# A ninth pair in place of two wide chunks, and x divided by its rms only in finished chunks

## The chip, the cores and the metric

The kernel runs on one core of one Trainium2 chip. The metric is the device time of one execution in microseconds (us), the median of several runs. Five engines matter here: PE (TensorE, matmuls), DVE (VectorE), ACT (ScalarE), POOL (GpSimd) and SP, which only issues DMAs. Each engine works through its own queue in order; semaphores make one engine wait for another.

## What is computed

One layer of a hybrid decoder block: 256 tokens, model width 4096. x is divided by its rms per token and multiplied by a gain per column; one input projection gives 27 column groups (queries, keys, values and gates of two attention mixers); each mixer's output is normalised, multiplied by SiLU of its gate columns, and the two go through an output projection onto the residual.

```
def _rmsnorm(x, g):
    y = x * rsqrt(mean(x * x, axis=-1) + 1e-6)          # one factor per token
    return y * g                                        # one factor per column
h = _rmsnorm(x, norm_g)
proj = h @ w_in                                         # 4096 -> 26 x 512 + 304 columns
q_a, k_a, v_a, z_a, q_b, kc, vc, ksl, vsl, kwn, vwn, z_b, g_b = split(proj)
o_a = dilated_mixture(q_a, k_a, v_a)                    # 16 heads of 128
o_b = nsa(q_b, kc, vc, ksl, vsl, kwn, vwn, sigmoid(g_b))
y = concat(_rmsnorm(o_a, out_g_a) * silu(z_a), _rmsnorm(o_b, out_g_b) * silu(z_b))
out = _rmsnorm(x + y @ w_out, final_g)
```

Since the rms is one factor per token, (x g / rms) @ w equals ((x g) @ w) / rms: the division can be made on x or on a finished column group.

## The kernel before

**Split products.** Every float32 factor is split into a high and a low part; a product is three matmuls (mm3, lines 98 to 100). ACT makes the high part and DVE the low part (split_to, lines 105 to 109). x comes transposed, as 32 k tiles of 128 columns x 256 tokens, in xh and xl.

**Stages.** Stage 1 (run_stream) multiplies x by single column groups, called chunks: a wide chunk has 512 columns and takes 32 k tiles x 2 token halves x 3 = 192 matmuls. Before the change it has five: 20 (kvc), 21 (sel) and 12 (za0), each 512 wide, then kw (256) and vg (304). Weights come in units of 1 MB through three buffers ("stage") and are split two k tiles at a time, for a 512 wide chunk, into three buffers ("split"); the code lets the splits run two such pieces ahead of the matmuls. While chunk 20 runs, x itself is split too (split_x); the squares of x are summed in the four units that follow (square_x), and token_rms makes rstd, the factor 1/rms per token.

**Pairs.** Stage 2 (run_pairs) multiplies two chunks at once by a block scheme with seven instead of eight products, for nine of the sixteen pairs of k tiles (FAST = 1); the other seven are done plainly. A pair so takes 9 x 21 + 7 x 24 = 357 matmuls of 512 columns. The seven products need sums of 128 x 128 blocks of x, made once in stage 1 (sum_blocks, split_sums, run as a task between the matmuls). There are eight pairs; banks go to DRAM through ACT (L473) and accumulating DMAs of POOL (put_sums). The first pair's buffers lie over those of stage 1. In this stage the order of the queues is written out by hand (manual_schedule); elsewhere a planner of the framework orders each queue by priorities and costs of its own.

**Where the division stands.** Chunks 20, 21, 12 and kw are multiplied by rstd as they leave PSUM (evict_away, L586). For all that follows x is loaded a second time (xr), multiplied by the gain and by a row of 1/rms (token_rms_rows: a matmul, L183, spreads rstd over the partitions), its block sums are made from that, and renew_x splits it into xh and xl again during the kw chunk.

**Stage 3** multiplies seven z chunks and the first output chunk, with the attention of both mixers as tasks between the matmuls. A head group of mixer A (attend_a) splits its values, then fetches its keys from DRAM (fetch, tag "qk" with two buffers: the keys take the values' buffer, so SP issues the DMA when the split is done), then transposes queries and keys on PE (L610). The next head group's values and queries are fetched early. attend_b fetches qb0 in start_b and transposes it next.

Of the kernel before, what the change touches and what calls it, by code (L numbers as in the profile page):

```python
# [83 lines left out]
def hybrid_trunk(ctx: ExitStack, tc: tile.TileContext, a: dict):  # L84
# [47 lines left out]
    def load_xT(piece):  # L132
# [4 lines left out]
        t = x_raw[piece] = room["o"].tile([P, G4, SEQ], F32, name="xp", tag="o", bufs=4)  # L137
# [19 lines left out]
    def load_x_nat(i):  # L157
        m, q = divmod(i, 4)
        t = x_nat[i] = room["o"].tile([P, DM // 4], F32, name="xn", tag="o", bufs=4)
        nc.sync.dma_start(t, a["x"][m * P : (m + 1) * P, q * DM // 4 : (q + 1) * DM // 4])  # L160
# [9 lines left out]
    def token_rms():  # L170
        s = room["work"].tile([P, NT], F32, name="ss")
        nc.vector.reduce_sum(s, ssx, axis=AX.X)
        rsqrt_mean(rstd, s, DM)
        dg = K["dg"] = room["work"].tile([P, NT, P], F32, name="dg", tag="xg")
        for m in range(NT):
            nc.vector.tensor_scalar_mul(dg[:, m], ident, rstd[:, m : m + 1])
        K["full"] = room["work"].tile([P, P], F32, name="full", tag="st")
        nc.vector.memset(K["full"], 1.0)

    def token_rms_rows():  # L180

        pr = room["psm"].tile([P, SEQ], F32, name="pr", tag="ps")
        nc.tensor.matmul(pr, K["full"], K["dg"].rearrange("p m t -> p (m t)"), start=True, stop=True)  # L183
        rows = K["rows"] = room["work"].tile([P, 1, SEQ], F32, name="rows", bufs=1)
        nc.scalar.activation(rows[:, 0], pr, AF.Copy)


    xn, sops, x_again = {}, {}, {}
# [6 lines left out]

    def sum_blocks(i):

        q, j = divmod(i, 4)
        if j == 0:
            xn[q] = room["o"].tile([P, 4, 2, SEQ], F32, name="xn", tag="o", bufs=4)  # L200
        if i % 2 == 0:
            t = x_again[i // 2] = room["work"].tile([P, G4, SEQ], F32, name="xr", tag="xr")
            nc.sync.dma_start(t, a["xT"][i // 2])
        t = x_again[i // 2]
        g = room["work"].tile([P, 2, SEQ], F32, name="xg", tag="xg")
        for d in range(2):
            nc.scalar.activation(g[:, d], t[:, 2 * (i % 2) + d], AF.Copy, scale=g_in[:, 2 * i + d : 2 * i + d + 1])
        n = xn[q][:, j]
        nc.vector.tensor_tensor(n, g, K["rows"].to_broadcast([P, 2, SEQ]), op=OP.mult)
        if FAST[i]:  # L210
            a11, a21, a12 = n[:, 0, :P], n[:, 0, P:], n[:, 1, :P]
            a22 = n[:, 1, P:]
            s = room["work"].tile([P, 4, P], F32, name="st", tag="st")
            add_blocks(s, a11, a12, a21, a22)
            sops[i] = s
# [8 lines left out]
    def sums():  # L224
        for i in range(NKP + 1):
            if i < NKP:
                sum_blocks(i)
            if i > 0:
                split_sums(i - 1)
            yield  # L230

    def renew_x(i):

        q, j = divmod(2 * i, QK)
        n = xn[i // 4][:, i % 4]
        split_to(xh[q][:, j : j + 2], xl[q][:, j : j + 2], n)
# [175 lines left out]
    IN_PLACES, IN_BANKS = ("f0", "t", "w", "p", "f1"), ("p6", "p7", "p5", "p4", "p1", "p2", "p3", "e")  # L412
# [163 lines left out]
    def fetch(key, width=CW):  # L576
        t = room["zq"].tile([P, NT, width], F32, name="fetched", tag="qk", bufs=2)
        nc.sync.dma_start(t, scratch(key))
        return t

    def evict_away(key, width=CW, func=AF.Copy, normal=False):

        def done(ps):
            t = room["ev"].tile([P, NT, width], F32, name="away", tag="ev", bufs=3)
            for m in range(NT):
                nc.scalar.activation(t[:, m], ps[m][:, :width], func, scale=1.0 if normal else rstd[:, m : m + 1])  # L586
# [812 lines left out]
```

## Time and profile before

| | |
|---|---|
| median of 3 runs | 1659.88 us (1655.72 to 1660.87) |
| the profiled execution | 1656.62 us, span 1654.8 us |
| PE / DVE / ACT / POOL busy | 98% / 82% / 61% / 8% |
| DMA | 388.04 MB, mean 234 GB/s |

The span reaches from the first to the last instruction of the profiled execution; its own time holds 1.8 us more. Busy PE is modelled (an instruction's end overlaps the next one's start), so paces are read from the starts of instructions.

### The profile page before, as it was taken

How to read it: one execution, taken by the hardware profiler on the slowest of the kernel's cores; microseconds unless marked ns; L12 is line 12 of the kernel's file. 1: busy time of each engine (PE TensorE's matmuls, PEld its weight loads, DVE VectorE, ACT ScalarE, POOL GpSimd, SP SyncE). 2: the span in 40 equal slices, each digit the busy share in tenths (PEclk: the TensorE clock that was granted, in tenths of full speed). 3: DMA queues.
4: the chain of work that ended last, by engine and by line, in shares of the span. 5: the costliest groups of instructions: out<-in, count | busy, mean ns of one | idle time of the engine just before them, and what ended most of it. 6: DMA issues, size and time to landing. Idle time of an engine off the chain costs nothing.

```text
span 1654.8 us, 20979 instructions
## 1 busy us (share of the span) xinstructions
PE 1623.2 (98%) x7772; PEld 1338.6 (81%) x7772; DVE 1354.5 (82%) x1665; ACT 1012.7 (61%) x1291; POOL 138.1 (8%) x183
## 2 busy tenths in 40 slices
PE   9999999999999999999999999999999999999997
PEld 6888978788888888888877787888888878878887
DVE  6586689989898989898966788987866769898984
ACT  6676556665665565656555767676666746656554
POOL 0000000111111111111120000000000000112110
PEclk9999999999999999999999999999999999999999
DMA  9785756979797978887889454544365456798974
GB/s 358 286 317 178 235 200 217 274 245 269 246 270 240 264 254 258 256 258 246 268 294 336 165 205 147 212 140 140 128 211 179 177 200 206 230 271 249 293 284 174
DMA packets 102519, 388.04 MB, mean 234 GB/s; under 512 B 12240, under 2 KB 12880, under 8 KB 88976
## 3 DMA queue, kind: packets, MB, share of 16 engines
q1 hardware_dynamic: 80064, 336.61, 57.6%
q0 software_dynamic: 21920, 49.03, 13.5%
q8 instruction: 61, 1.00, 0.2%
q10 hardware_dynamic: 432, 1.05, 0.2%
q14 instruction: 42, 0.34, 0.1%
HBM read 338.36 MB, written 50.38 MB: 235 GB/s over the span
## 4 chain that ended last, share of the span: by engine, by line
PE 84%; DVE 6%; DMA 3%; issue 3%; ACT 3%; SPq 0%; ACTq 0%; POOLq 0%; POOL 0%; DVEq 0%
PE p L99 14%; PE p L100 13%; PE p L98 13%; PE acc L99 11%; PE acc L100 11%; PE acc L98 10%; PE e L100 2%; PE e L99 2%; PE e L98 2%; DVE bf L459 2%; DMA bw<-in_w_in 1%; DMA w<-in_cmp_v_w 1%; DVE bf L458 1%; DVE bt L452 1%; PE pt L1030 1%
## 5 line engine op out<-in xcount | busy, mean ns | idle before, releaser
L106 DVE TENSOR_TENSOR wl<-w,wh 128x1024 fp32r<-128x1024 f32 (+2 forms) x210 | 246.8, 1178 | 132.0 <-ACT wh L105 131.6
L105 ACT ACTIVATE wh<-w 128x1024 fp32r<-128x1024 f32 (+2 forms) x210 | 214.5, 1024 | 154.6 <-PE acc L100 132.1
L98 PE MATMUL acc<-wh,xh 128*128 128x512 f32 (+2 forms) x768 | 293.8, 383 | 2.6 <-ACT wh L105 2.6
L99 PE MATMUL acc<-wl,xh 128*128 128x512 f32 (+2 forms) x768 | 292.4, 381 | 1.5 <-DVE wl L106 1.5
L100 PE MATMUL acc<-wh,xl 128*128 128x512 f32 (+2 forms) x768 | 291.7, 380 | 0.0
L459 DVE TENSOR_TENSOR bf<-bt,bf 128x2048 fp32r<-128x2048 f32 x99 | 226.1, 2284 | 0.0
L454 ACT ACTIVATE bf<-bt 128x1024 fp32r<-128x1024 f32 x99 | 104.9, 1059 | 170.7 <-DVE bt L452 170.7
L106 DVE TENSOR_TENSOR bp<-bw,bp 128x2048 fp32r<-128x2048 f32 x66 | 151.0, 2288 | 64.8 <-ACT bp L105 64.8
L451 ACT ACTIVATE bf<-bw 128x1536 fp32r<-128x1536 f32 x99 | 147.0, 1485 | 62.4 <-DMA bw<-in_w_in 39.5
L105 ACT ACTIVATE bp<-bw 128x2048 fp32r<-128x2048 f32 x66 | 126.0, 1909 | 78.1 <-PE e L100 63.2
L458 DVE TENSOR_TENSOR bf<-bw,bf 128x1536 fp32r<-128x1536 f32 x99 | 173.3, 1751 | 0.0
L98 PEld LDWEIGHTS acc<-wh,xh 128*128 128x128 f32 x768 | 145.3, 189 | 27.1 <-ACT wh L105 3.8
L99 PEld LDWEIGHTS acc<-wl,xh 128*128 128x128 f32 x768 | 145.4, 189 | 26.7 <-DVE wl L106 3.5
L100 PEld LDWEIGHTS acc<-wh,xl 128*128 128x128 f32 x768 | 145.3, 189 | 24.4
L457 ACT ACTIVATE bf<-bt 128x1024 fp32r<-128x1024 f32 x99 | 105.2, 1063 | 38.7 <-DVE bt L456 37.9
L452 DVE TENSOR_TENSOR bt<-bw 128x1024 f32<-128x1024 f32 x99 | 120.9, 1221 | 9.7 <-DMA bw<-in_w_in 6.5
L99 PE MATMUL p<-bf,sum 128*128 128x512 f32 x288 | 113.2, 393 | 2.9 <-DVE bf L459 2.9
L100 PE MATMUL p<-bf,sum 128*128 128x512 f32 x288 | 112.3, 390 | 0.0
L98 PE MATMUL p<-bf,sum 128*128 128x512 f32 x288 | 112.3, 390 | 0.0
L99 PE MATMUL p<-bp,xh 128*128 128x512 f32 x288 | 112.2, 389 | 0.0
L98 PE MATMUL p<-bp,xh 128*128 128x512 f32 x288 | 112.0, 389 | 0.0
L100 PE MATMUL p<-bp,xl 128*128 128x512 f32 x288 | 112.0, 389 | 0.0
(329 smaller groups left out, 3295.3 us busy)
## 6 DMA issues: line engine op xcount, KB each, us to landing
bw<-in_w_in SPq DMA_DIRECT2D x256, 512.0 KB, 6.1
w<-in_w_in SPq DMA_DIRECT2D x76, 1024.0 KB, 5.0
bw<-in_w_out SPq DMA_DIRECT2D x96, 512.0 KB, 5.1
w<-in_w_out SPq DMA_DIRECT2D x16, 1024.0 KB, 5.0
scr_q<-parts POOLq DMA_DIRECT2D x30, 256.0 KB, 7.3
scr_k<-parts POOLq DMA_DIRECT2D x30, 256.0 KB, 7.7
scr_v<-parts POOLq DMA_DIRECT2D x30, 256.0 KB, 7.7
scr_qb<-parts POOLq DMA_DIRECT2D x30, 256.0 KB, 8.9
```

Of the source, the lines that this page charges most:

```text
L98: nc.tensor.matmul(out, lh, rh, start=start, stop=False)
L99: nc.tensor.matmul(out, lh, rl, start=False, stop=False)
L100: nc.tensor.matmul(out, ll, rh, start=False, stop=stop)
L105: nc.scalar.activation(h, src, AF.Copy)
L106: nc.vector.tensor_sub(l, src, h.bitcast(F32))
L451: nc.scalar.activation(h[:, :3], w[:, B22:], AF.Copy)
L452: nc.vector.tensor_tensor(t[:, T3 : T1 + 1], w[:, B22 : B11 + 1], w[:, B12 : B12 + 1].to_broadcast([P, 2, CW]), op=OP.subtract)
L454: nc.scalar.activation(h[:, 3:5], t[:, T3 : T1 + 1], AF.Copy)
L457: nc.scalar.activation(h[:, 5:], t[:, T2:], AF.Copy)
L458: nc.vector.tensor_sub(l[:, :3], w[:, B22:], h[:, :3].bitcast(F32))
L459: nc.vector.tensor_sub(l[:, 3:], t, h[:, 3:].bitcast(F32))
L1030: nc.tensor.transpose(pt[:rows, j], src, ident)
```

## The change

Stage 1 keeps only the chunks 20, kw and vg; 21 and 12 become a ninth pair, the last of stage 2. x is no longer renewed: xh and xl stay x times gain, without the division, in all stages. The block sums are made from the first load of x (x_raw, now with eight buffers) while chunk 20 runs, by one ACT and four DVE instructions for each of the nine fast k pairs; the second load, the spreading matmul and renew_x go away. The division moves to the finished chunks: queries, keys and sel are multiplied by rstd on POOL after they are fetched (divide=True: two instructions of 128 x 512 each, for 13 fetches), values in split_values, z chunks inside the Silu, vg at its eviction. za0, which used to pass Silu in stage 1, passes it in gate after its fetch. The pace of the tasks, the order of PSUM banks and the place of token_rms change with it.

```
--- before.py
+++ after.py
@@ -134,7 +134,7 @@
         if half == 0:
             xh.append(big.tile([P, QK, SEQ], F32R, name=f"xh{q}", tag="x", bufs=8))
             xl.append(big.tile([P, QK, SEQ], F32R, name=f"xl{q}", tag="x", bufs=8))
-        t = x_raw[piece] = room["o"].tile([P, G4, SEQ], F32, name="xp", tag="o", bufs=4)
+        t = x_raw[piece] = room["o"].tile([P, G4, SEQ], F32, name="xp", tag="o", bufs=8)
         if piece == 0:
             nc.sync.dma_start(g_in, a["norm_g"])
             for j, e in ((0, 1), (1, 2), (2, 4)):
@@ -156,7 +156,7 @@
 
     def load_x_nat(i):
         m, q = divmod(i, 4)
-        t = x_nat[i] = room["o"].tile([P, DM // 4], F32, name="xn", tag="o", bufs=4)
+        t = x_nat[i] = room["work"].tile([P, DM // 4], F32, name="xn", tag="xn", bufs=4)
         nc.sync.dma_start(t, a["x"][m * P : (m + 1) * P, q * DM // 4 : (q + 1) * DM // 4])
 
     def square_x(i):
@@ -171,21 +171,9 @@
         s = room["work"].tile([P, NT], F32, name="ss")
         nc.vector.reduce_sum(s, ssx, axis=AX.X)
         rsqrt_mean(rstd, s, DM)
-        dg = K["dg"] = room["work"].tile([P, NT, P], F32, name="dg", tag="xg")
-        for m in range(NT):
-            nc.vector.tensor_scalar_mul(dg[:, m], ident, rstd[:, m : m + 1])
-        K["full"] = room["work"].tile([P, P], F32, name="full", tag="st")
-        nc.vector.memset(K["full"], 1.0)
-
-    def token_rms_rows():
-
-        pr = room["psm"].tile([P, SEQ], F32, name="pr", tag="ps")
-        nc.tensor.matmul(pr, K["full"], K["dg"].rearrange("p m t -> p (m t)"), start=True, stop=True)
-        rows = K["rows"] = room["work"].tile([P, 1, SEQ], F32, name="rows", bufs=1)
-        nc.scalar.activation(rows[:, 0], pr, AF.Copy)
-
-
-    xn, sops, x_again = {}, {}, {}
+
+
+    sops = {}
 
     def add_blocks(s, a11, a12, a21, a22):
         nc.vector.scalar_tensor_tensor(s[:, 0], a21, -1.0, a22, op0=OP.mult, op1=OP.subtract)
@@ -193,26 +181,22 @@
         nc.vector.tensor_tensor(s[:, 2], a11, a21, op=OP.subtract)
         nc.vector.tensor_tensor(s[:, 3], a12, s[:, 1], op=OP.subtract)
 
+    minus_g = cst.tile([P, KT], F32, name="minus_g")
+
     def sum_blocks(i):
 
-        q, j = divmod(i, 4)
-        if j == 0:
-            xn[q] = room["o"].tile([P, 4, 2, SEQ], F32, name="xn", tag="o", bufs=4)
-        if i % 2 == 0:
-            t = x_again[i // 2] = room["work"].tile([P, G4, SEQ], F32, name="xr", tag="xr")
-            nc.sync.dma_start(t, a["xT"][i // 2])
-        t = x_again[i // 2]
-        g = room["work"].tile([P, 2, SEQ], F32, name="xg", tag="xg")
-        for d in range(2):
-            nc.scalar.activation(g[:, d], t[:, 2 * (i % 2) + d], AF.Copy, scale=g_in[:, 2 * i + d : 2 * i + d + 1])
-        n = xn[q][:, j]
-        nc.vector.tensor_tensor(n, g, K["rows"].to_broadcast([P, 2, SEQ]), op=OP.mult)
-        if FAST[i]:
-            a11, a21, a12 = n[:, 0, :P], n[:, 0, P:], n[:, 1, :P]
-            a22 = n[:, 1, P:]
-            s = room["work"].tile([P, 4, P], F32, name="st", tag="st")
-            add_blocks(s, a11, a12, a21, a22)
-            sops[i] = s
+        if not FAST[i]:
+            return
+        k = 2 * i
+        r1, r2 = x_raw[i // 2][:, k % G4], x_raw[i // 2][:, k % G4 + 1]
+        a22 = room["work"].tile([P, P], F32, name="a22", tag="a22")
+        nc.scalar.activation(a22, r2[:, P:], AF.Copy, scale=g_in[:, k + 1 : k + 2])
+        s = sops[i] = room["work"].tile([P, 4, P], F32, name="st", tag="st")
+        m1 = minus_g[:, k : k + 1]
+        nc.vector.scalar_tensor_tensor(s[:, 0], r1[:, P:], m1, a22, op0=OP.mult, op1=OP.subtract)
+        nc.vector.scalar_tensor_tensor(s[:, 1], r1[:, :P], m1, s[:, 0], op0=OP.mult, op1=OP.subtract)
+        nc.vector.tensor_tensor(s[:, 2], a22, s[:, 1], op=OP.subtract)
+        nc.vector.scalar_tensor_tensor(s[:, 3], r2[:, :P], g_in[:, k + 1 : k + 2], s[:, 1], op0=OP.mult, op1=OP.subtract)
 
     def split_sums(i):
         if FAST[i]:
@@ -222,18 +206,14 @@
             sops[i] = t
 
     def sums():
-        for i in range(NKP + 1):
-            if i < NKP:
-                sum_blocks(i)
-            if i > 0:
-                split_sums(i - 1)
-            yield
-
-    def renew_x(i):
-
-        q, j = divmod(2 * i, QK)
-        n = xn[i // 4][:, i % 4]
-        split_to(xh[q][:, j : j + 2], xl[q][:, j : j + 2], n)
+        nc.vector.tensor_scalar_mul(minus_g, g_in, -1.0)
+        fast = [i for i in range(NKP) if FAST[i]]
+        for n in range(len(fast) + 1):
+            if n < len(fast):
+                sum_blocks(fast[n])
+            if n > 0:
+                split_sums(fast[n - 1])
+            yield
 
 
     tasks = deque()
@@ -409,7 +389,7 @@
 
     B12, B22, B11, B21 = range(4)
     T3, T1, T2, T4 = range(4)
-    IN_PLACES, IN_BANKS = ("f0", "t", "w", "p", "f1"), ("p6", "p7", "p5", "p4", "p1", "p2", "p3", "e")
+    IN_PLACES, IN_BANKS = ("f0", "t", "w", "p", "f1"), ("p5", "p1", "p2", "p4", "p6", "p7", "p3", "e")
     OUT_PLACES, OUT_BANKS = ("f1", "t", "p", "f0", "w"), ("p7", "p1", "p6", "p5", "p4", "p2", "p3", "e")
 
     def run_pairs(w_src, dcs, lhs_of, sops, begin, places, names, out=False):
@@ -573,17 +553,19 @@
             scr[key] = dram.tile([P, NT, width], F32, name=f"scr_{key}")
         return scr[key]
 
-    def fetch(key, width=CW):
+    def fetch(key, width=CW, divide=False):
         t = room["zq"].tile([P, NT, width], F32, name="fetched", tag="qk", bufs=2)
         nc.sync.dma_start(t, scratch(key))
+        for m in range(NT if divide else 0):
+            nc.gpsimd.tensor_scalar_mul(t[:, m], t[:, m], rstd[:, m : m + 1])
         return t
 
-    def evict_away(key, width=CW, func=AF.Copy, normal=False):
+    def evict_away(key, width=CW):
 
         def done(ps):
             t = room["ev"].tile([P, NT, width], F32, name="away", tag="ev", bufs=3)
             for m in range(NT):
-                nc.scalar.activation(t[:, m], ps[m][:, :width], func, scale=1.0 if normal else rstd[:, m : m + 1])
+                nc.scalar.activation(t[:, m], ps[m][:, :width], AF.Copy, scale=rstd[:, m : m + 1])
             nc.sync.dma_start(scratch(key, width), t)
         return done
 
@@ -591,7 +573,7 @@
 
         v = room["work"].tile([P, NT, 4, 2, HD], F32R, name="va", tag="n", bufs=2)
         for m in range(NT):
-            split_to(v[:, m, :, 0], v[:, m, :, 1], src[:, m].rearrange("p (j d) -> p j d", j=4))
+            split_to(v[:, m, :, 0], v[:, m, :, 1], src[:, m].rearrange("p (j d) -> p j d", j=4), rstd[:, m : m + 1])
         return v
 
     def transposed(src, key, scale=None):
@@ -645,14 +627,14 @@
     def attend_a(hg):
         vsrc, qsrc = st.pop("va"), st.pop("qa")
         v = split_values(vsrc)
-        ksrc = fetch(f"k{hg}")
+        ksrc = fetch(f"k{hg}", divide=True)
         yield
         yield from transposed(qsrc, "qa", SCALE)
         yield from transposed(ksrc, "ka")
         if hg < 3:
-            st["va"], st["qa"] = fetch(f"v{hg + 1}"), fetch(f"q{hg + 1}")
+            st["va"], st["qa"] = fetch(f"v{hg + 1}"), fetch(f"q{hg + 1}", divide=True)
         else:
-            st["sel"], st["kw"] = fetch("sel"), fetch("kw", 2 * HD)
+            st["sel"], st["kw"] = fetch("sel", divide=True), fetch("kw", 2 * HD)
         qh, ql = st["qaT"]
         kh, kl = st["kaT"]
         o_tiles("a")
@@ -730,6 +712,9 @@
                 nc.sync.dma_start(sz[m], scratch(f"z{which}{i}")[:, m])
             yield
             yield
+            if (which, i) == ("a", 0):
+                for m in range(NT):
+                    nc.scalar.activation(sz[m], sz[m], AF.Silu, scale=rstd[:, m : m + 1])
         for m in range(NT):
             ys = o_at(which, i * CW, CW)[:, m]
             nc.vector.scalar_tensor_tensor(ys, ys, r[:, m : m + 1], sz[m], op0=OP.mult, op1=OP.mult)
@@ -747,7 +732,7 @@
         def done(ps):
             sz = [room["zq"].tile([P, CW], F32, name="sz", tag="zt", bufs=4) for m in range(NT)]
             for m in range(NT):
-                nc.scalar.activation(sz[m], ps[m], AF.Silu)
+                nc.scalar.activation(sz[m], ps[m], AF.Silu, scale=rstd[:, m : m + 1])
             if which in finished:
                 tasks.appendleft(gate(which, i, sz))
             else:
@@ -812,7 +797,7 @@
                 nc.tensor.transpose(pt[:, g, m], t[:, m, c0 : c0 + HD], ident)
         nc.scalar.activation(tT, pt, AF.Copy)
         if which == 1:
-            st["va"], st["qa"] = fetch("v0"), fetch("q0")
+            st["va"], st["qa"] = fetch("v0"), fetch("q0", divide=True)
         pe = room["work"].tile([P, CBL], F32, name="pe", tag="pe", bufs=2)
         nc.sync.dma_start(pe, a[f"cmp_{n}_pe"])
         w2 = room["zq"].tile([P, 2, HD], F32, name="w2", tag="zt", bufs=4)
@@ -935,7 +920,7 @@
         yield
         put_v(0, sel[:, :, 2 * HD :])
         yield
-        st["qb"] = fetch("qb0")
+        st["qb"] = fetch("qb0", divide=True)
         put_v(1, vg[:, :, : 2 * HD])
         g2 = B["gates"]
         nc.scalar.activation(g2, vg[:, :, 2 * HD :], AF.Exp, scale=-1.0)
@@ -946,7 +931,7 @@
     def attend_b(hg):
         yield from transposed(st.pop("qb"), "qb", SCALE)
         if hg < 3:
-            st["qb"] = fetch(f"qb{hg + 1}")
+            st["qb"] = fetch(f"qb{hg + 1}", divide=True)
         first, second = attend_half(hg, 0), attend_half(hg, 1)
         for _ in range(5):
             next(first)
@@ -1209,19 +1194,15 @@
         room[name] = opened(inner, name, n)
 
     room["apart"].tile([P, 3 * HID], F32, name="apart")
-    psum = banks(4, 3, 1)
+    psum = banks(6, 1, 1)
     room["first"] = True
     first_ps, last_ps = [], []
-    pace = 0.5
-    add_chunk(w_chunk(20), CW, x_lhs, first_ps.extend)
-    add_chunk(w_chunk(21), CW, x_lhs, evict_away("sel"), pace=pace)
-    add_chunk(w_chunk(12), CW, x_lhs, evict_away("za0", func=AF.Silu), pace=pace)
-    add_chunk([a["w_kw"][g] for g in range(4)], 2 * HD, x_lhs, evict_away("kw", 2 * HD))
-    add_chunk([a["w_vg"][g] for g in range(8)], 2 * HD + NGATE, x_lhs, last_ps.extend)
-    hooks[1, 17] = token_rms
-    hooks[1, 20] = lambda: (token_rms_rows(), evict_away("kvc")(first_ps), tasks.append(sums()))
-    for i in range(NKP):
-        hooks[3, 2 * i + 1] = lambda i=i: renew_x(i)
+    add_chunk(w_chunk(20), CW, x_lhs, first_ps.extend, pace=0.4)
+    add_chunk([a["w_kw"][g] for g in range(4)], 2 * HD, x_lhs, evict_away("kw", 2 * HD), pace=0.8)
+    add_chunk([a["w_vg"][g] for g in range(8)], 2 * HD + NGATE, x_lhs, last_ps.extend, pace=0.8)
+    hooks[0, 14] = lambda: tasks.append(sums())
+    hooks[1, 26] = token_rms
+    hooks[1, 28] = lambda: evict_away("kvc")(first_ps)
     run_stream()
     while tasks:
         advance()
@@ -1231,7 +1212,7 @@
     room["pairs"] = opened(inner, "pairs", 1)
 
     def begin_pairs():
-        evict_away("vg", 2 * HD + NGATE, normal=True)(last_ps)
+        evict_away("vg", 2 * HD + NGATE)(last_ps)
         psum.close()
         room["banks"] = opened(psum, "banks", 1, space=PS)
         right.close()
@@ -1242,6 +1223,7 @@
         for n, c in (("q", 0), ("k", 4), ("v", 8)):
             dcs.append(((c + i, c + i + 1), (f"{n}{i}", f"{n}{i + 1}")))
         dcs.append(((16 + i, 17 + i), (f"qb{i}", f"qb{i + 1}")))
+    dcs.append(((21, 12), ("sel", "za0")))
     ordered = ExitStack()
     ordered.enter_context(tc.manual_schedule())
     rest = run_pairs(a["w_in"], dcs, x_lhs, sops, begin_pairs, IN_PLACES, IN_BANKS)
```

## Rows read from the trace of the kernel before

**Rows 1.** The page, busy time of PE.
```profile
PE 1623.2 (98%) x7772; PEld 1338.6 (81%) x7772; DVE 1354.5 (82%) x1665; ACT 1012.7 (61%) x1291; POOL 138.1 (8%) x183
```
**Rows 2.** What PE waited for, whole span: total us, times, longest.
```profile
PE p L99 <- DVE bf L459: 5.4, 5, 1.2
```
**Rows 3.** Busy time by stretch in stage 1: stretch, length, engines, clock, DMA.
```profile
30.00:40.00 10.00, 10.00 (x45) 8.02 (x44) 7.22 (x12) 6.78 (x11) 0.00 (x0) 1.00 0.98 390
40.00:50.00 10.00, 10.00 (x44) 8.07 (x43) 7.08 (x11) 5.80 (x10) 0.00 (x0) 1.00 0.82 305
50.00:60.00 10.00, 10.00 (x44) 8.03 (x44) 4.59 (x4) 6.82 (x10) 0.00 (x0) 1.00 0.97 364
...
90.00:100.00 10.00, 10.00 (x45) 8.02 (x44) 9.88 (x23) 9.01 (x16) 0.00 (x0) 1.00 0.82 272
```
**Rows 4.** PE in order of time: last of chunk 12, kw, pairs.
```profile
144.68 0.40 PE L98 MATMUL acc<-wh,xh 128*128 128x512 f32 x1
...
147.96 0.40 PE L100 MATMUL acc<-wh,xl 128*128 128x512 f32 x1
148.19 0.28 PE L98 MATMUL acc<-wh,xh 128*128 128x256 f32 x1
...
197.86 0.40 PE L98 MATMUL p<-bf,xh 128*128 128x512 f32 x1
```
**Rows 5.** ACT in order of time: a pair's last bank leaves PSUM.
```profile
281.77 0.60 ACT L473 ACTIVATE parts<-e 128x512 f32<-128x512 f32 x1 [0.34 <-PE e L100]
...
365.58 0.60 ACT L473 ACTIVATE parts<-e 128x512 f32<-128x512 f32 x1 [0.76 <-PE e L100]
...
446.53 0.60 ACT L473 ACTIVATE parts<-e 128x512 f32<-128x512 f32 x1 [0.76 <-PE e L100]
```
**Rows 6.** PE's groups in the first 240 us: the spreading matmul.
```profile
L183 PE MATMUL pr<-dg,full 128*128 128x256 f32 x2 | 0.6, 380 | 0.0
```
**Rows 7.** DVE's groups by form, first 200 us: one sum, its split.
```profile
L106 DVE TENSOR_TENSOR sum<-st,sum 128x512 fp32r<-128x512 f32 x9 | 6.2, 687 | 1.0 <-ACT sum L105 0.8
...
L191 DVE SCALAR_TENSOR_TENSOR st<-xn 128x128 f32<-128x128 f32 x9 | 2.5, 283 | 0.0
```
**Rows 8.** One piece of chunk 20 being split: ACT, then DVE.
```profile
35.50 1.06 ACT L105 ACTIVATE wh<-w 128x1024 fp32r<-128x1024 f32 x1 [0.55 <-PE acc L100]
...
36.59 1.22 DVE L106 TENSOR_TENSOR wl<-w,wh 128x1024 fp32r<-128x1024 f32 x1 [0.39 <-ACT wh L105]
```
**Rows 9.** SP's fetch issues, and PE's transposes of what was fetched.
```profile
950.98 0.32 SPq L578 DMA_DIRECT2D fetched<-scr_k  x1
...
954.90 1.04 PE L610 MATMUL pt<-ident,fetched 128*128 128x128 f32 x8
...
999.87 0.33 SPq L578 DMA_DIRECT2D fetched<-scr_k  x1
...
1006.17 1.03 PE L610 MATMUL pt<-ident,fetched 128*128 128x128 f32 x8
...
1043.59 0.42 SPq L578 DMA_DIRECT2D fetched<-scr_qb  x1
...
1050.06 1.06 PE L610 MATMUL pt<-ident,fetched 128*128 128x128 f32 x8
```
**Rows 10.** DMA issues: count, size, median us from issue to landing.
```profile
fetched<-scr_k SPq DMA_DIRECT2D x4, 512.0 KB, 3.4
fetched<-scr_qb SPq DMA_DIRECT2D x4, 512.0 KB, 5.5
```
**Rows 11.** POOL's groups by form, whole span: its arithmetic on two elements.
```profile
L115 POOL TENSOR_TENSOR roa<-rsq,nhalf 128x2 f32<-128x2 f32 x1 | 0.7, 722 | 152.8 <-DVE rsq L114 152.8
```
**Rows 12.** Busy time by stretch in stage 3, columns as in rows 3.
```profile
940.00:960.00 20.00, 19.89 (x114) 16.75 (x115) 17.91 (x42) 17.23 (x34) 0.00 (x0) 1.00 0.57 202
...
1040.00:1060.00 20.00, 19.88 (x106) 16.53 (x104) 19.47 (x51) 11.59 (x28) 0.00 (x0) 1.00 0.85 307
```

## The prediction

> **What bounds the kernel now.** I read the page first: PE is busy 98% of the span [rows 1], and no other engine comes near. Busy PE is a model, so I looked next at what PE waited for: its largest group of waits is 5.4 us in five pieces [rows 2], nothing against 1655 us. So time moves when PE gets fewer matmuls, or when something new makes it wait. The views by stretch and by order of time then give the price of each. In stage 1 PE has no idle time after the first 16 us, while DVE stands between 4.59 and 9.88 of 10 us [rows 3]; in 90 to 100, where the block sums are made, DVE is full and PE still does not wait. The reader should take from this that a full DVE alone costs nothing here as long as the splits stay ahead of PE.
>
> **Two chunks become a pair.** Two wide chunks are 384 matmuls. From 144.68 to 147.96 are 14 steps, 0.2343 us each [rows 4], so they take 384 x 0.2343 = 90.0 us, and stage 1 gets that much shorter. A pair in full swing takes 446.53 - 365.58 = 80.95 us from one last bank to the next [rows 5]. That is 357 matmuls of 0.2268 us: the pair saves 27 matmuls, and each one of its own is 0.0075 us quicker than in stage 1, for whatever reason. The ninth pair comes last and finds the others running, so I price it at 80.95. What it does on ACT (sums, evictions), POOL (16 accumulating DMAs) and DVE lies inside that period already. Gain 90.0 - 80.95 = 9.0 us. If it ran at stage 1's pace it would be 357 x 0.2343 = 83.6 us, and the gain 6.4. The first pair took 281.77 - 197.86 = 83.9 us [rows 4, 5], so entering stage 2 costs some 3 us. The new layout of stage 1's buffers under the first pair's may change that by as much either way; the last of them that PE reads are the split buffers, as before, so I take no change.
>
> **What goes away with the renewal.** The spreading matmul is 0.6 us of busy PE at most [rows 6]; with its overlap I take 0.4. The second load of x, 32 gain activations, 16 multiplications by the row and 16 renewing splits ran beside a PE that did not wait, so they are worth nothing. The sums keep their four DVE instructions and their split; only the place changes. Together 9.4 us.
>
> **The sums in chunk 20.** They start behind k tile 14. Chunk 20 ends at 148.19 - 90.0 - 0.4 = 57.8, 17 tiles of 6 x 0.2343 = 1.41 us earlier is 33.9 us. A sum costs DVE 4 x 0.283 + 0.687 = 1.82 us [rows 7], and at a pace of 0.4 about eight of nine come before 57.8: 14.6 us. DVE's idle time there is 6.1 x 0.28 + 10 x 0.29 + 7.8 x 0.54 = 8.8 us [rows 3]. So it is over by 5.8 us at worst. The splits have a lead: a piece whose buffer PE left at 35.5 is done at 37.8 [rows 8], and PE wants it two pieces of 2.81 us behind that, at 41.1, 3.3 us later. So PE loses at most 2.5 us. At least it loses nothing, since means of such short instructions hold the overlap with the next, and the planner may put splits first, as it did at 90 to 100 [rows 3]. I take 0.5, near the lower end, for that row. What waits behind a late split is PE's piece and nothing else; DVE has recovered in kw, where no x is split. token_rms and the eviction of kvc now stand in kw; the squares they wait for come from the four units of kw, as long as those of chunk 21, so I see nothing late.
>
> **POOL multiplies what was fetched.** This is the part that can cost. The fetched keys of a head group are wanted by PE as they land: issue 950.98, landing after 3.4 us at 954.4, transposes at 954.90, a slack of 0.5 us; the third head group repeats this. For the fourth it is 999.87 + 3.4 = 1003.3 against 1006.17, 2.9 us; for qb0 1043.59 + 5.5 = 1049.1 against 1050.06, 1.0 us [rows 9, 10]. The first head group's keys have more, and the other eight divided fetches are issued a head group ahead. At these four places two POOL instructions of time T now stand between landing and PE. Behind them in POOL's queue are other such multiplications and a small pow; POOL's bank DMAs of the last pair stand ahead, as now. The loss, if PE's order stays as it is, is L(T) = 2 max(0, 2T - 0.5) + max(0, 2T - 2.9) + max(0, 2T - 1.0).
>
> T is not in the trace. POOL's arithmetic on 2 elements takes 0.72 us [rows 11], a lower bound; DVE's on 128 x 512 takes 0.69 [rows 7], so 0.72 + 0.69 = 1.41 when POOL is as fast by element as DVE. If it must also wait for one DVE split of 1.22 [rows 8] it is 2.63. L is 2.3 at 0.72, 4.0 at 1.0, 6.5 at 1.41 and 16.1 at 2.63. I take T = 1.0, between the two bare ends. Below all this is nothing: stage 3 is ordered by the planner, which knows of the new instructions and can put matmuls of the z chunk before the transposes. I take half of 4.0, 2.0 us.
>
> [...]
>
> DVE and POOL could also get in each other's way: DVE is busy 17.91 of 20 us in 940 to 960 and 19.47 in 1040 to 1060 [rows 12]; four POOL instructions fall in each. At 0.7 us for each meeting DVE has 2.8 us more to do against 2.1 and 0.5 idle, so this adds up to 3 us of DVE time, and PE's lead covers some. I leave it in the range. [...] Before the change POOL did almost no arithmetic, so the trace cannot say. [...]
>
> za0's Silu adds two activations and a change of ACT's table and back to a stretch where ACT is busy 11.59 of 20 us [rows 12]; the eight idle us hide it. The factor in split_values, the z chunks and vg adds no instruction.
>
> **Sum.** -9.4 + 0.5 + 2.0 = -6.9 us: span 1654.8 to 1647.9, the profiled execution 1656.6 to 1649.7. The median of the three runs is 3.3 us above that execution, so the median forecast is 1659.9 - 6.9 = 1653.0.
>
> **The rivals.** First, nothing is lost: the planner hides POOL, and chunk 20 holds. Then -9.4, 1650.5. For it speaks that PE did not wait in stage 3 for any fetch; against it the slack of 0.5.
>
> Second, the gain goes to POOL's waits: PE's order stays, and T is 1.0 to 2.3. At T = 1.41 it is -9.4 + 0.5 + 6.5 = -2.4, 1657.5: no change. For it speaks that PE takes the keys right behind their landing.
>
> Third, slower: POOL's multiplication is held up by DVE's instructions each time. The sum passes +5 us when L passes 13.9, at 8T - 4.9 = 13.9, T = 2.35. At 2.63 it is -8.9 + 16.1 = +7.2, 1667.1. Against it: only two places have no slack, and not every moment of DVE is a split.
>
> Fourth, the change saves less because the ninth pair runs at stage 1's pace: -9.4 + 2.6 + 2.5 = -4.3, 1655.6.
>
> **How the numbers follow.** About 0.3%, 5 us, is what a measurement of this kernel can tell from no change. Chances: the forecast (-5 to -8.5) 0.42, nothing lost 0.20, POOL's waits on PE's path 0.25, the slower pair 0.05, slower 0.08. Faster gets the first two, 0.62; same 0.30; slower 0.08. The likeliest case's own range is 1651.4 to 1655. The whole range reaches down to nothing lost with 3 us of the entry into stage 2, 1647.5, and up to POOL's waits with T near 1.8 (L = 9.5, +0.6), 1660.5.
>
> **What would show it.** The step of a pair stays 80.95 for the ninth; stage 2 begins 90 us earlier, near 107.5; in 34 to 58 DVE is at 9 of 10 or more and PE's starts stay 0.234 apart, or show gaps up to 2.5 us in all; in stage 3 PE waits for POOL at the second and third head group and at qb0, in all 1 to 4 us; POOL's multiplications take 0.7 to 1.4 us. The prediction is wrong if POOL's instructions take over 2 us, if chunk 20 stalls by more than 3 us, or if entering stage 2 costs more than 6 us.

## The result, and the profile after

The changed kernel takes 1671.72 us (median of 4 runs, 1671.26 to 1676.31) against 1657.8 us for the kernel before in the same measurement: ratio 1.0086, 95% interval 1.0069 to 1.0102. It is slower by 14 us. The forecast was 1653.0, with 1660.5 as the upper end of the range: wrong in sign and outside the range.

The profiled execution is the longest of the four (1676.31 us, span 1674.4). Its page, line of the engines, answers to [rows 1]: PE's busy share fell by one point, POOL's rose from 8 to 12%.

```profile
PE 1621.6 (97%) x7743; PEld 1334.6 (80%) x7743; DVE 1375.1 (82%) x1651; ACT 1011.5 (60%) x1259; POOL 197.4 (12%) x224
```

What PE waited for (total us, times, longest) has a new first line. Against [rows 2]:

```profile
PE pt L592 <- POOL fetched L560: 12.0, 8, 2.7
PE p L99 <- DVE bf L439: 7.7, 7, 1.2
PE ph L842 <- DVE bhl L106: 5.6, 2, 3.0
PE acc L99 <- DVE wl L106: 4.1, 6, 1.5
PE acc L98 <- ACT wh L105: 4.0, 3, 1.8
```

The places of the landmarks show where to look. In order of time, the last bank of the eighth and of the ninth input pair and of the first output pair leave through ACT (the rows that answer to [rows 5]):

```profile
766.52 0.60 ACT L453 ACTIVATE parts<-e 128x512 f32<-128x512 f32 x1 [0.51 <-PE e L100]
847.48 0.60 ACT L453 ACTIVATE parts<-e 128x512 f32<-128x512 f32 x1 [0.76 <-PE e L100]
1449.82 0.60 ACT L453 ACTIVATE parts<-e 128x512 f32<-128x512 f32 x1 [0.37 <-PE e L100]
```

In the kernel before, the same output bank:

```profile
1431.78 0.60 ACT L473 ACTIVATE parts<-e 128x512 f32<-128x512 f32 x1 [0.76 <-PE e L100]
```

The ninth pair takes 847.48 - 766.52 = 80.96 us. Stage 2 ended at 852.05 before and ends at 847.48 now: 4.6 us are gained up to there, and in the other kernels below that keep this part, 6 to 10. From there to the end of the first output pair, which I call stage 3, it is 1431.78 - 852.05 = 579.7 us before and 602.3 now. Of what was lost, 22.6 us was lost in stage 3; behind its end 1.6 us more go (1674.4 - 1449.82 = 224.6 us against 1654.8 - 1431.78 = 223.0).

In stage 1 the block sums did what was hoped for. The stretches while chunk 20 runs with the block sums in it (columns as in [rows 3]): DVE is full, PE does not wait.

```profile
30.00:40.00 10.00, 10.00 (x44) 8.04 (x43) 10.00 (x21) 8.28 (x17) 0.00 (x0) 1.00 0.94 358
40.00:50.00 10.00, 10.00 (x45) 8.03 (x44) 9.75 (x22) 9.07 (x17) 0.00 (x0) 1.00 0.72 264
50.00:60.00 10.00, 10.00 (x47) 8.16 (x46) 9.96 (x21) 7.52 (x13) 0.00 (x0) 1.00 0.90 338
```

Stage 3 is where POOL now stands between a landed tile and PE. POOL's multiplications (ns, shortest/median/longest; first and last start):

```profile
L560 POOL TENSOR_SCALAR fetched<-fetched,rstd x26: 1557/1568/3647, 889.4 to 1117.2; 128x512 f32<-128x512 f32 x26
```

Around the second head group's keys POOL's queue and then PE's show the chain. The keys land, POOL needs 3.98 us for its two instructions, and PE's transposes (L592) follow each of them, with one matmul of the z chunk (951.74) between:

```profile
949.14 3.98 POOL L560 TENSOR_SCALAR fetched<-fetched,rstd 128x512 f32<-128x512 f32 x2 [16.91 <-DMA fetched<-scr_k]
```

```profile
948.93 0.39 PE L100 MATMUL acc<-wh,xl 128*128 128x512 f32 x1
951.54 0.44 PE L592 MATMUL pt<-ident,fetched 128*128 128x128 f32 x2 [2.22 <-POOL fetched L560]
951.74 0.48 PE L98 MATMUL acc<-wh,xh 128*128 128x512 f32 x1
953.17 1.05 PE L592 MATMUL pt<-ident,fetched 128*128 128x128 f32 x6 [0.96 <-POOL fetched L560]
...
955.52 0.63 PE L99 MATMUL acc<-wl,xh 128*128 128x512 f32 x1
955.94 0.63 PE L100 MATMUL acc<-wh,xl 128*128 128x512 f32 x1
956.37 0.63 PE L98 MATMUL acc<-wh,xh 128*128 128x512 f32 x1
956.80 0.56 PE L99 MATMUL acc<-wl,xh 128*128 128x512 f32 x1
957.19 0.40 PE L100 MATMUL acc<-wh,xl 128*128 128x512 f32 x1
```

The reader is to see a second thing here: behind the wait, matmuls of 512 columns start 0.42 us apart instead of 0.234. From 954.0 to 957.2, where they stand, the granted clock is 0.51; from 957.2 to 960, where such matmuls start 0.23 us apart again, it is 1.00. In the windows around the four places (clock in the third column from the end) the granted clock is below 1 in three of them.

```profile
950.00:960.00 10.00, 7.50 (x32) 6.15 (x33) 5.19 (x9) 2.98 (x6) 4.46 (x3) 0.83 0.60 188
980.00:990.00 10.00, 7.12 (x37) 5.41 (x36) 4.03 (x5) 3.81 (x6) 3.19 (x2) 1.00 0.69 243
1010.00:1020.00 10.00, 7.68 (x34) 5.98 (x33) 4.30 (x8) 3.50 (x9) 6.76 (x4) 0.83 0.62 196
1060.00:1070.00 10.00, 6.70 (x24) 5.66 (x25) 5.30 (x10) 3.19 (x4) 7.14 (x5) 0.66 0.61 206
```

That is 1.7 + 1.7 + 3.4 = 6.8 us of full clock taken away in these windows, a part of them while PE waited anyway.

### The profile page after: what moved, and what is told of

It reads as the page before. It is cut to its first block, busy times and chain, and to the rows that moved or that the text cites. A ratio compares the mean times of both kernels' runs of the same rounds, so it can differ in the third digit from the quotient of the medians.

```text
span 1674.4 us, 20936 instructions
## 1 busy us (share of the span) xinstructions
PE 1621.6 (97%) x7743; PEld 1334.6 (80%) x7743; DVE 1375.1 (82%) x1651; ACT 1011.5 (60%) x1259; POOL 197.4 (12%) x224
## 4 chain that ended last, share of the span: by engine, by line
PE 74%; DVE 10%; DMA 6%; issue 5%; ACT 3%; POOL 1%; SPq 0%; ACTq 0%; POOLq 0%; DVEq 0%
PE p L99 14%; PE p L100 13%; PE p L98 13%; PE acc L99 8%; PE acc L100 7%; PE acc L98 7%; DMA bw<-in_w_in 3%; DVE bf L439 2%; PE e L100 2%; PE e L99 2%; PE e L98 2%; DVE bf L438 2%; DVE bt L432 1%; DVE wl L106 1%; DMA w<-in_cmp_v_w 1%
## 5 line engine op out<-in xcount | busy, mean ns | idle before, releaser
L106 DVE TENSOR_TENSOR wl<-w,wh 128x1024 fp32r<-128x1024 f32 (+2 forms) x178 | 209.0, 1176 | 111.1 <-ACT wh L105 110.5
L105 ACT ACTIVATE wh<-w 128x1024 fp32r<-128x1024 f32 (+2 forms) x178 | 180.6, 1018 | 128.4 <-PE acc L100 100.7
L98 PE MATMUL acc<-wh,xh 128*128 128x512 f32 (+2 forms) x640 | 243.3, 382 | 4.0 <-ACT wh L105 4.0
L99 PE MATMUL acc<-wl,xh 128*128 128x512 f32 (+2 forms) x640 | 242.7, 379 | 4.2 <-DVE wl L106 4.1
L100 PE MATMUL acc<-wh,xl 128*128 128x512 f32 (+2 forms) x640 | 241.4, 377 | 0.0
L99 PEld LDWEIGHTS acc<-wl,xh 128*128 128x128 f32 x640 | 122.1, 191 | 23.9 <-DVE wl L106 7.2
L98 PEld LDWEIGHTS acc<-wh,xh 128*128 128x128 f32 x640 | 121.8, 191 | 22.8 <-ACT wh L105 5.5
L100 PEld LDWEIGHTS acc<-wh,xl 128*128 128x128 f32 x640 | 121.7, 190 | 18.7
L99 PE MATMUL p<-bf,sum 128*128 128x512 f32 x324 | 127.7, 394 | 5.3 <-DVE bf L439 5.2
L98 PE MATMUL p<-bf,sum 128*128 128x512 f32 x324 | 126.3, 390 | 0.0
L100 PE MATMUL p<-bf,sum 128*128 128x512 f32 x324 | 126.2, 390 | 0.0
L99 PE MATMUL p<-bp,xh 128*128 128x512 f32 x324 | 126.1, 389 | 0.0
L98 PE MATMUL p<-bp,xh 128*128 128x512 f32 x324 | 126.0, 389 | 0.0
```

The costliest lines, as they stand in the source:

```text
L98: nc.tensor.matmul(out, lh, rh, start=start, stop=False)
L99: nc.tensor.matmul(out, lh, rl, start=False, stop=False)
L100: nc.tensor.matmul(out, ll, rh, start=False, stop=stop)
L105: nc.scalar.activation(h, src, AF.Copy)
L106: nc.vector.tensor_sub(l, src, h.bitcast(F32))
```

## The experiments

Three theories stood in the expectations. P: PE waits for POOL's product of keys and qb0, and loses what follows each wait. C: POOL's reads of SBUF hold up DVE wherever they stand. N: the ninth pair or the new stage 1 is what got slower. "The changed kernel" is the base of each edit.

For all kernels together: the median, the ratio to the kernel before (95% interval), and of one profiled execution each the end of stage 2, the length of stage 3, PE's waits in stage 3 (sum of that view), and the time the low clock took there (for each 10 us of stage 3, 10 x (1 - granted clock), summed). All times in us. Kernels were measured in several rounds, each beside the kernel before; "by the ratios" below is the difference of two ratios times 1658 us. Outside stage 2 the planner orders the queues anew for every kernel, so a difference of a few us between two of them can also be its order; no run holds that order fixed.

```
kernel            median   ratio                    end 2  stage 3  waits  clock
before            1657.8                            852.1   579.7   11.2    3.4
changed           1671.72  1.0086 [1.0069, 1.0102]  847.5   602.3   26.7    8.7
e1_no_divide      1654.98  0.9985 [0.9972, 0.9998]  843.9   582.9   12.9    3.4
e2_act_divide     1654.03  0.9974 [0.9960, 0.9989]  843.8   582.2   13.8    1.7
e3_dve_divide     1651.8   0.9966 [0.9953, 0.9979]  843.8   581.7   13.2    3.5
e4_keys_early     1662.9   1.0027 [1.0011, 1.0042]  843.6   589.1   17.7    3.4
e5_early_qb_dve   1656.24  0.9985 [0.9976, 0.9995]  842.3   585.3   15.4    1.7
e6_eight_pairs    1661.35  1.0021 [1.0011, 1.0030]  853.3   584.7   13.5    6.8
e7_qb_dve         1667.99  1.0058 [1.0043, 1.0073]  844.5   596.1   22.8    6.8
e8_early_dve      1659.18  1.0003 [0.9992, 1.0014]  843.8   588.4   16.2    6.8
e9_path_dve       1656.79  0.9991 [0.9980, 1.0001]  844.7   589.4   16.2    8.5
e10_keys_twice    1676.13  1.0108 [1.0094, 1.0122]  844.0   606.1   28.9   12.0
e11_fill          1677.12  1.0104 [1.0086, 1.0122]  843.6   608.2   23.0    8.5
e12_pool_beside   1655.34  0.9982 [0.9971, 0.9992]  845.7   585.7   15.1    5.1
```

**e1, e2, e3: no multiplication, or one on another engine.** e1 drops the two lines; e2 and e3 change the engine:

```
-            nc.gpsimd.tensor_scalar_mul(t[:, m], t[:, m], rstd[:, m : m + 1])
+            nc.scalar.activation(t[:, m], t[:, m], AF.Copy, scale=rstd[:, m : m + 1])     # e2
+            nc.vector.tensor_scalar_mul(t[:, m], t[:, m], rstd[:, m : m + 1])             # e3
```

> The changed kernel without the 26 POOL multiplications: queries, keys and sel stay undivided, which this kernel leaves out; all else as changed. Theory P (PE waits for POOL's product of keys and qb0, 12.0 us in the changed kernel, and what follows each wait): stage 3 gets as short as before the change, the time falls to 1649 to 1654 us, below the kernel before. Rival N (stage 1 or the ninth pair is what got slower): it stays at 1664 or more. Rival C (POOL's reads hold up DVE wherever they stand) expects the same fall as P here; e4 tells it from P.

> The multiplications move from POOL to ACT, two activations with a scale per fetch, about 0.7 us each. P: the path from landing to PE keeps 1.4 us in place of 3.2 to 4, plus ACT's queue, which is some two thirds full; 1653 to 1661 us, between e1 and the changed kernel. C: as e1, since POOL is idle: 1649 to 1654. N: 1664 or more.

> The multiplications move to DVE, two instructions of 128x512 per fetch, 0.4 to 0.7 us each. P: the path from landing to PE keeps 0.8 to 1.4 us plus DVE's queue, which is nearly full in that stretch; 1653 to 1662 us. C: 1649 to 1656. N: 1664 or more.

All three come out below the kernel before, e3 at 1651.8 lowest. Of P's ranges, e1 lies 1.0 us above its own, e2 in its own and e3 1.2 us below. From the changed kernel to e3 it is 19.9 us, by 26 instructions that moved. N falls: stage 1 and the nine pairs are the same in all of them. In e3 the multiplications take a third of the time:

```profile
L560 DVE TENSOR_SCALAR fetched<-fetched,rstd x26: 469/480/489, 887.1 to 1114.8; 128x512 f32<-128x512 f32 x26
```

and two of the four windows above read, with PE at 9.77 and 10.00 of 10 and the full clock:

```profile
950.00:960.00 10.00, 9.77 (x53) 7.71 (x52) 8.61 (x26) 6.17 (x12) 0.00 (x0) 1.00 0.52 200
1060.00:1070.00 10.00, 10.00 (x57) 8.39 (x56) 9.96 (x33) 9.07 (x20) 0.00 (x0) 1.00 0.24 97
```

That e1, which does less, is not below e3 (the intervals overlap) shows that the multiplications themselves cost nothing measurable on DVE. They do not yet tell P from C, since in all three POOL multiplies nothing.

**e4, e5: POOL multiplies, but a head group ahead.** Keys and queries are fetched and multiplied one head group early and the values take the late place; e5 has qb0 on DVE besides.

```
     def attend_a(hg):
-        vsrc, qsrc = st.pop("va"), st.pop("qa")
-        v = split_values(vsrc)
-        ksrc = fetch(f"k{hg}", divide=True)
-        yield
+        qsrc, ksrc = st.pop("qa"), st.pop("ka")
         yield from transposed(qsrc, "qa", SCALE)
+        vsrc = fetch(f"v{hg}")
         yield from transposed(ksrc, "ka")
...
+        yield
+        v = split_values(vsrc)
+        if hg < 3:
+            st["ka"] = fetch(f"k{hg + 1}", divide=True)
...
+            (nc.vector if key == "qb0" else nc.gpsimd).tensor_scalar_mul(t[:, m], t[:, m], rstd[:, m : m + 1])   # e5
```

> POOL still makes all 26 multiplications, but of each head group the keys and queries are fetched a head group ahead, with the same two buffers, and the values, which POOL does not touch, come on the path in their place; in start_b sel is used before kw, so that qb0 is fetched earlier. P: PE's waits for POOL fall from 12.0 us to under 3, and the time to 1649 to 1657 us. C: POOL's reads still meet DVE's, the time stays at 1662 or more. N: 1664 or more.

> As e4_keys_early (keys and queries fetched a head group ahead and multiplied by POOL), but qb0, for whose product by POOL PE still waited 3.4 us there, is multiplied by DVE; 24 of the 26 multiplications stay on POOL, all off PE's path. Theory P (only what PE waits for costs): the time falls to e3's, 1650 to 1656 us. Rival C (POOL's reads hold up DVE wherever they stand): it stays at 1658 or more, as e4.

e4 falls to 1662.9, 8.8 us below the changed kernel. By its time that is C's range (1662 or more) and not P's; its waits for POOL fell as P had it, nearly (3.4 us, under 3 expected), and are those of qb0 alone:

```profile
PE pt L592 <- POOL fetched L560: 3.4, 2, 2.5
```

In e5 they are gone, and with 24 of 26 multiplications still on POOL the median is 1656.24, below the kernel before. That is 0.2 us above P's range and 1.8 below C's: the place in the chain is most of what costs, as P has it, while by C 24 of 26 parts of the 17 to 20 us would have stayed. e8 below shows where the rest of e4 comes from.

**e7, e9: DVE for a part of the path, in the changed order.** e7 moves qb0 alone to DVE, e9 all that PE takes as it lands (k0 to k3 and qb0); the other 16 stay on POOL.

```
+            (nc.vector if key == "qb0" else nc.gpsimd).tensor_scalar_mul(...)                        # e7
+            (nc.vector if key[0] == "k" or key == "qb0" else nc.gpsimd).tensor_scalar_mul(...)       # e9
```

> The changed kernel with one fetch altered: qb0 is multiplied by DVE, the other twelve by POOL, keys on PE's path as changed. P: what qb0 costs goes, a wait of some 4 us and the slow clock behind it, 3 us more: 1662 to 1667 us; the three waits for keys stay. C: two POOL instructions of 26 fewer, 1669 to 1672 us.

> The changed kernel with DVE for the five fetches whose product PE waits for (the keys of four head groups and qb0), and POOL for the other eight (queries, sel, later qb), 16 instructions. Order of fetches as changed. Theory P (only the products on PE's path cost): as e3, 1650 to 1655 us. Rival C (POOL's reads hold up DVE wherever they stand): 16 of 26 of the loss of 17 to 20 us stays, 1660 or more.

qb0 alone gives 3.7 us (4.6 by the ratios, whose intervals overlap a little), 1.0 us above P's range and 1.0 below C's; in the changed kernel PE's starts at qb0 lose 4.0 us against their usual steps. The waits for POOL go from 12.0 to 7.2 us, but the clock still fell behind 1064 (3.4 us). e9 gives 14.9 us. No wait for POOL is left in it; the largest new one is

```profile
PE s L98 <- ACT kaT L105: 2.8, 1, 2.8
```

and the clock takes 8.5 us, more than in e3. Its median stays 5.0 us above e3's, between P's range and C's. What makes these 5 us was not separated: 3.0 us of waits and 5.0 of low clock fill them in the profile.

**e8: the early order with everything on DVE.** The order of e4, the engine of e3.

> Both remedies: keys and queries fetched a head group ahead, and all divisions on DVE. P: little is left to win over e3, 1649 to 1654 us. C says nothing here, since POOL is idle. A third reading, that the values now on the path are late, would show as 1655 or more.

P's range is missed and the third reading's met. At 1659.18 it is 7.4 us slower than e3 (6.1 by the ratios), and no quicker than e5, which has 24 of the 26 on POOL. The early order therefore has a price of its own, without any POOL: PE waits 2.6 us once for ACT's oT and 3.6 us for DVE's n. So the remainder of e4 and e5 above e3 need not be POOL's: at this order e4, with all 26 on POOL, is 3.7 us above e8 (intervals overlap), with 3.4 us of waits for POOL.

**e10: the keys multiplied twice.**

```
+            if key[0] == "k":
+                nc.gpsimd.tensor_scalar_mul(t[:, m], t[:, m], 1.0)
```

> The changed kernel with a second POOL multiplication, by 1.0, behind each one of the keys: the suspected cost doubled, eight POOL instructions more. P: each of three or four head groups waits 3.1 to 4 us longer, and the clock stays low longer: 1682 to 1692 us. C: eight POOL instructions of 34, 26 of which cost 17 to 20: 1676 to 1678 us.

4.4 us more by the medians, 3.6 by the ratios, whose intervals overlap; P had expected 10 to 20. The time itself lies in C's range. The waits:

```profile
PE pt L594 <- POOL fetched L562: 12.8, 6, 3.8
...
PE pt L594 <- POOL fetched L560: 3.0, 2, 1.9
```

15.8 us instead of 12.0. The direction is P's, the size is not: eight more instructions of 1.57 us did not add their sum. A part of the reason stands in PE's rows: at the second to fourth head group the last matmul ahead of the keys' transposes starts 1.1, 1.6 and 1.5 us after POOL begins with these keys (945.99 against 944.88 at the second), in the changed kernel 0.2 and 0.7 us before it and 0.3 us after. More of the other matmuls stood there, and the expectation left that out. C does not explain the 4.4 us either: DVE's instructions were held up as much as in the changed kernel (4.1 and 3.8 us, see e12).

**e11: idle matmuls in front of the transposes**, to fill the wait and hold the clock.

```
+            for _ in range(10):
+                nc.tensor.matmul(fill, idle[:, :P], idle, start=True, stop=True)
```

> The changed kernel with ten idle matmuls of 128x512 in bf16 (2.1 us of PE work on zeros, nothing reads them) in front of the transposes of the keys, four times, and of the first qb: 10.7 us of PE work more. If PE really idles there and the low clock behind the waits costs time of its own, they fill the wait and the granted clock in the stretches behind it stays at 1.00: 1665 to 1670 us, faster than the changed kernel though PE has more to do. If the clock costs nothing: 1671 to 1674 us. If PE does not idle there: 1680 to 1683 us.

It misses all three ranges. The first of the five fills holds PE from 918.01 to the next start at 920.16, 2.15 us, and the rows of the five last 2.32 or 2.33 us each; the waits for POOL are still 9.8 us, the clock lost 8.5 us as before (8.7), and the median rose by 5.4 us (3.0 by the ratios, with overlapping intervals). The price of the low clock by itself was not separated by it.

**e12: e3 with POOL working beside it.** POOL multiplies 384 columns of each tile into a tile that nobody reads.

```
+            nc.vector.tensor_scalar_mul(t[:, m], t[:, m], rstd[:, m : m + 1])
+            side = room["work"].tile([P, 384], F32, name="side", bufs=1)
+            nc.gpsimd.tensor_scalar_mul(side, t[:, m, :384], rstd[:, m : m + 1])
```

> As e3_dve_divide (all divisions on DVE), and POOL also multiplies 384 of the 512 columns of every tile that DVE has divided, 26 instructions of its own, into a tile that nobody reads: POOL's reads of SBUF stand beside DVE's work as in the changed kernel, but nothing waits for them. Theory P (only products that PE waits for cost): as e3, 1650 to 1655 us. Rival C (POOL's reads hold up DVE wherever they stand, which would also explain the 5 us by which e9 stays behind e3): 1656 or more, and DVE's instructions of two SBUF inputs last longer while POOL works.

1655.34 against 1651.8 for e3: 2.7 us by the ratios, whose intervals overlap, and 6.5 from end to end of the intervals. That is 0.3 us above P's range and 0.7 below C's, and bounds what C is worth here, with POOL reading three quarters of what it reads in the changed kernel. The instructions do meet: POOL's shortest takes 1.24 us, its longest 5.08:

```profile
L562 POOL TENSOR_SCALAR side<-fetched,rstd x26: 1242/1414/5080, 889.7 to 1121.2; 128x384 f32<-128x384 f32 x26
```

How much DVE is held up can be read directly, from its splits between 850 and 1130 us. First the changed kernel, then e3, where POOL multiplies nothing:

```profile
L106 DVE TENSOR_TENSOR wl<-w,wh x59: 1161/1224/1630, 849.0 to 1123.8; 128x1024 fp32r<-128x1024 f32 x59
L106 DVE TENSOR_TENSOR wl<-w,wh x64: 1160/1221/1227, 853.6 to 1129.6; 128x1024 fp32r<-128x1024 f32 x64
```

Counted over all instructions of DVE of 0.1 us or more between 880 and 1125 us that last over 0.06 us longer than the median of their form: none in the kernel before, e1, e2, e3, e6 and e8, where POOL multiplies nothing; 16 in the changed kernel, which add up to 3.8 us; 4.2 us in e4, 4.7 in e5, 2.8 in e9, 1.7 in e12. Each of them overlaps a multiplication of POOL. So what C says of DVE is there (that it is POOL's reads that do it was not shown), but in all it takes 3.8 us of DVE's time, not 20 of PE's, and e5, which has more of it than the changed kernel, is 15 us faster.

**e6: e3 with eight pairs.** Chunks 21 and 12 go back into stage 1; no renewal, division in finished chunks.

```
+    add_chunk(w_chunk(21), CW, x_lhs, evict_away("sel"))
+    add_chunk(w_chunk(12), CW, x_lhs, evict_away("za0"))
...
-    dcs.append(((21, 12), ("sel", "za0")))
```

> As e3_dve_divide (all divisions on DVE), but with the ninth pair undone: chunks 21 and 12 stand in stage 1 again as wide chunks, multiplied by rstd as they leave PSUM. By the sum of the prediction the pair is worth 9.0 us: 1660 to 1662 us, and stage 2 ends at 852 us, not at 844. Rival N (the pair saves nothing, and the gain of e3 is the work of the renewal that went away): 1650 to 1654 us.

1661.35 against 1651.8: the ninth pair in place of the two chunks is worth 9.5 us (9.1 by the ratios). It also shows that the other parts of the change together (no renewal of x, division in finished chunks, here on DVE) gain nothing: against the kernel before the ratio is 1.0021. The edit also puts the banks of the pairs in another order and leaves sel and za0 to be divided at their eviction.

## Why the prediction was wrong, step by step

**Two chunks become a pair: right.** Predicted 9.0 us with a ninth pair of 80.95; measured 9.5 between e3 and e6, and 80.96. Stage 2 ends 8.1 to 8.4 us earlier in e1 to e4. In the changed kernel's own profile it is 4.6, with 7.7 us of waits for bf against about 5.3 in most others; no part of the change accounts for that. Pairs begin at 108.98 where 107.5 was forecast; the 1.5 us stand ahead of the end of chunk 20 (kw begins at 59.31, not 57.8) and no wait in 30 to 60 makes them. They arise earlier: in 10 to 20 PE is busy 6.47 of 10 us, before the change 8.97. kw begins late in e1 and e3 too (58.85 and 59.30), so this goes with the new stage 1; the prediction has no term for it, and which part of the new stage makes it was not tried.

**The sums in chunk 20: right, at the lower end.** 0.5 us predicted, 2.5 at most; no wait was seen with DVE at 9.75 to 10.00.

**What goes away with the renewal: the sign is open.** 0.4 us predicted. e6 is 0.1 to 0.3% slower than the kernel before. In its profile stage 3 is 5.0 us longer; waits (2.3) and the clock (3.4) make that up. Which of the scaled split of values, za0's Silu, the multiplications on DVE or another order by the planner brings the waits was not tried.

**POOL multiplies what was fetched: this step failed.** It had 2.0 us; stage 3 of the changed kernel is 20.6 us longer than that of e3. Three things were off.

First, T. I took 1.0 from a range of 0.72 to 1.41 for an instruction that nothing holds up, by the rows of a two-element operation and of DVE. The shortest of the 26 takes 1.56, the median 1.57, above that bound: it stood on POOL being as fast by element as DVE. The longest takes 3.65.

Second, the planner. I halved L because it could put other matmuls before the transposes. In the changed kernel it did not: L(1.57) is 2 x 2.64 + 0.24 + 2.14 = 7.7 us, and PE waited 12.0, at just the four places that the prediction names. With what the pairs of instructions really took there (4.00, 3.22, 3.70 and 5.20 us), the same sum is 3.50 + 2.72 + 0.80 + 4.20 = 11.2. So 7.7 us are the lone instruction, 3.5 its stretching beside DVE, and nothing was taken off for the planner. In [rows 9] the transposes stand right behind the landing, and in the rows of PE above right behind each product, with one matmul put between the two.

Third, what follows a wait. The prediction knew only the wait itself: with 12.0 in place of 2.0 its sum gives 1663.0, and 8.7 us are still missing. In the three windows the clock took up to 6.8 us more. Over e3, the changed kernel's stage 3 has 13.5 us more waits and 5.2 us more of low clock, 18.7 of the 20.6; e10 has 15.7 + 8.5 = 24.2 of 24.4; e7 9.6 + 3.3 = 12.9 of 14.4. Only e4 and e5 leave about 3 us over. That the waits bring the clock down is argued from the order in time, not shown: e7 and e9 kept falls where a wait for POOL was gone, e9 has 5.0 us more of low clock than e3 with 3.0 us more of waits, and the kernel before has 3.4 us of falls too. What brings the clock down stays open.

**The rivals.** Nothing lost, 1650.5, is what e3 comes near to with another engine. The fourth, a slower ninth pair, falls with 80.96. The second, POOL's waits on PE's path, was the right mechanism, with a chance of 0.25. Its T went from 1.0 to 2.3, and the mean on the path, 2.01, lies in that; but it was priced at 1.41 alone, 1657.5, and the range was closed at T = 1.8. At 2.3 the same sum gives L = 13.5 and 1664.5, still 7 us short. The third, slower because POOL's multiplication is held up by DVE each time, had the right place, sign and nearly the size (1667.1 at T = 2.63), with a chance of 0.08. The size is in part luck: of the waits some 3.5 us are the stretching beside DVE, while the shortest instruction is too long already, and the clock, which it does not know, made up the rest. Beside each other both last longer: POOL's 1.57 become up to 3.65 us, and a DVE split that takes 1.22 us takes up to 1.63. T = 2.63 supposes that POOL waits for all of a split; the other way round no such full wait shows: a split that began 0.27 us into a multiplication of 1.56 us (991.85 in the changed kernel) took only 0.27 us longer. The 0.7 us for each meeting was my estimate, and no run shows it: the 16 instructions of DVE that lasted longer in the changed kernel lost 3.8 us together, 0.24 each. Off PE's path e5 and e12 bound the worth of this to a few us; it matters through the length of the POOL instruction that PE waits for. The prediction's own sign that it would be wrong (POOL's instructions over 2 us) came true for six of the 26, all beside work of DVE.

The best version is e3, the changed kernel with these 26 instructions on DVE: 1651.8 us, ratio 0.9966 [0.9953, 0.9979]. That it lies so near the forecast of 1653.0 is in part luck: without its POOL term the sum is -8.9 us, while e3 is 5.6 us below the kernel before (by the ratios 9.1 gained by the pair, 3.5 lost by the rest of the change).

## What to carry to other kernels

Where PE takes a tile as it lands, an instruction put in between can be paid in full: two of 1.57 us or more on POOL were, all but the 0.5 us of slack, two of 0.48 on DVE cost nothing that could be measured. An engine that has not been seen with that shape is to be priced well above the engine it is likened to (here 1.57 us were measured where I took 1.0 and the likeness to DVE gave 1.41), and nothing is to be taken off for a planner that may make room: here it did not. Idle share is no reason to choose an engine: here the one with 8% busy before the change cost 20 us, and the one with 82% nothing; its instruction was a third as long. Behind waits of PE of 2 to 4 us read the granted clock of the window too: in the changed kernel, e7 and e10 another 0.3 to 0.5 us of low clock came with each us of wait over e3, though that the one makes the other is not shown.

## What was not expected of the hardware

- DVE multiplies 128 x 512 by one factor per row in 0.48 us (e3), where its two-input operation of that size takes 0.69. The ratio is 0.70. POOL's same instruction takes 1.57, 3.3 times DVE's.
- An instruction of POOL of one shape took up to 2.3 times its shortest (1.56 to 3.65 us), the one of 384 columns up to 4.1 times (1.24 to 5.08).
- The granted clock falls for a few us in every profile of this kernel, in all from 1.7 to 12.0 us of full clock in stage 3; the most where PE's waits are the most (e10).
